# Few-row products become transfers, transposes or zero-padded products; meta keys turned four heads at a time

## The chip, the cores and the metric

The kernel runs on one core of a Trainium2 chip. The metric is device microseconds of one execution. A core has TensorE (PE in the profile; its weight loads are PEld), VectorE (DVE), ScalarE (ACT), GpSimd (POOL) and SyncE (SP); transfers are issued from the queues of SP, POOL and ScalarE.

## What is computed

The reference is a small model on one sequence: 256 tokens behind 16 meta tokens, width 1024, all in float32. Four blocks follow one another, each with a residual: (1) an attention with 16 heads of 64 over a window of 128 keys plus the 16 meta keys and a sink; (2) a gated delta rule with 8 key heads and 16 value heads of 128, run in chunks, so that the 16 meta tokens give a first state for the 256 others; (3) a mixer of a differential attention (4 heads) and a windowed attention (8 query heads on two heads of keys and values, seeing the meta keys too); (4) a SwiGLU feed-forward. In short:

```python
h = concat(meta_tokens, x)
h = h + attention_mixer(h, ...)          # block 1
h = h + deltanet_mixer(h, ...)           # block 2
h = concat(meta_tokens_2, h[16:])
h = h + mixer_block(rms_norm(h), ...)    # block 3
h = h + swiglu(rms_norm(h), ...)         # block 4
return rms_norm(h)[16:]
```

## The kernel before

Activations lie transposed, with 128 features on the partitions and the 272 tokens along the free dimension. Weights come from HBM in pieces (`raw`), and each piece is split into a high part (`hi`, written by ScalarE) and a low part (`lo`, written by VectorE); a projection is three fast products per piece (`mm3`), into the PSUM banks `mm`. These products are most of TensorE's work (the names `mm<-U,hi` and `mm<-U,lo` in the profile). All other products are plain float32, through `Plan.mm` into the PSUM banks `aux`, where one product is two TensorE instructions; a transposition (`Plan.tr`) is one.

Every operation is recorded by a helper (`Plan._rec`, hence one line number, L223, for all), with an estimated duration. `Plan.schedule` then places all operations of the kernel in one order by priority, with an estimate of each engine's time, of buffers and of transfers; `Plan.emit` writes them out in that order, each engine in order. Buffers are rings by tag (`SLOTS`): a tile must be the next of its tag, or at most a few ahead (`AHEAD`), to be placed.

The places that the change touches, in the order of time:

- In `attention`, `V[:, 2, :]` holds the values of the 16 meta tokens (16 rows), and `VM` is to hold them once for each of two query blocks and two heads, shifted to rows 32b + 16e, so that one product with 128 rows serves a pair of heads (`pair`). Before, eight instructions with 16-row operands shift them, with a selection matrix `sel`, through PSUM.
- In `meta`, the attention of the 16 meta queries: the scores are products over 64 rows (one half of the partitions for each of two key heads), and the output is a product over 16 rows.
- In `gates`, `rstd` (the same in every row) is brought into token order by 1-row products with `self.unity`, and the cumulative sums of the gates of the meta tokens are products over 16 rows (`gt0`). The sums go to HBM (`mem<-row`) and come back to all partitions (`U<-mem`, `gb`), for `decays`.
- In `key_norms`, the scaled betas of the meta tokens (`br0`, 16x16) are transposed into `brow`.
- In `tokens(j)`, the keys of head j are transposed; the meta keys too, and then copied to two places of `kt0` with a scale for each head (16 copies of 16x128 in all). `first_states` multiplies `kt0` by `U0`, the inverses for the meta tokens, into `W0`, which each head's first product reads. In the order, `tokens` lie between 190 and 287 us, `first_states` beside the merges of the block inverses (`merge`) near 290 us.
- In `second_mixer`, `VM` is built as in the first attention, with two pairs of 16-row instructions.

Of the kernel before, what the change touches and what calls it, by code (L numbers as in the profile page):

```python
# [10 lines left out]
F32 = mybir.dt.float32  # L11
# [7 lines left out]
NM = 16  # L19
# [112 lines left out]
class Plan:  # L132
# [337 lines left out]
class Net:  # L470
# [10 lines left out]
    def constants(self):  # L481
# [17 lines left out]
        self.unity = self.eps[0:1, 2:3]  # L499
# [169 lines left out]
    def attention(self, h):  # L669
# [20 lines left out]
        V = p.tile([128, 3, 128], F32, "x1")  # L690
        vps = p.bank("aux")
# [6 lines left out]
        sel = p.tile([16, 4, 64], F32, "c")  # L698
        p.memset(sel, 0.0)
        VM = p.tile([128, 2, 128], F32, "vm")  # L700
        p.memset(VM, 0.0)
        for b in range(2):
            mps = p.bank("aux")
            for e in range(2):
                q = 2 * b + e
                p.copy(sel[:, q, 32 * b + 16 * e:32 * b + 16 * e + 16], self.ident[0:16, 0:16])
                p.mm(mps[0:64, 64 * e:64 * e + 64], sel[:, q, :], V[0:NM, 2, 64 * e:64 * e + 64])
            p.act(VM[0:64, b, :], mps[0:64, 0:128], AF.Copy)
# [38 lines left out]
        def meta():  # L747
            biasm = p.tile([128, 2, NM], F32, "c")
            p.dma(biasm, a["bias_m"], 16384, "gpsimd", after=(keys,))
            qm = p.tile([128, 8, NM], F32, "c")  # L750
            p.copy(qm, qT[:, :, 0:NM])
            t = p.tile([128, 2, NM], F32, "c")
            for e in range(2):
                es = slice(64 * e, 64 * e + 64)
                sps = p.bank("aux")[:, 0:NM]
                p.mm(sps, qm[es].rearrange("p j t -> p (j t)"), kT[es, 0:NM])
                p.tt(t[:, e, :], sps, biasm[:, e, :], ALU.add)
# [18 lines left out]
            pm = p.tile([NM, 256], F32, "x1")  # L776
            p.act(pm, pps[0:NM, 0:256], AF.Copy)
            ops = p.bank("aux")
            for e in range(2):
                ec = slice(64 * e, 64 * e + 64)  # L780
                p.mm(ops[ec, 0:128], V[0:NM, 2, ec], pm[:, 128 * e:128 * e + 128])
# [76 lines left out]
    def deltanet(self, h):  # L858
# [73 lines left out]
        id16 = self.ident[0:16, 0:16]  # L932
        beta, g = [p.tile([128, 3, 16], F32, "t3") for _ in range(2)]
        bt, bt0, gt, gt0 = beta[:, 0:2, :], beta[0:NM, 2, :], g[:, 0:2, :], g[0:NM, 2, :]
# [25 lines left out]
        for t in (U0, kt0):  # L960
            p.memset(t, 0.0)
# [6 lines left out]
        def gates():  # L968
# [18 lines left out]
            for t, (t0, w) in enumerate(KEY_TILES):  # L987
                p.mm(ps[0:w, 32 * t:32 * t + 32], rows[:, t0:t0 + w], fold)
                if t < 2:
                    p.mm(ps[:, 96 + t:97 + t], rstd[0:1, t0:t0 + w], self.unity)  # L990
# [3 lines left out]
            p.act(rt, ps[:, 96:98], AF.Copy)  # L994
# [23 lines left out]
            p.mm(ps[0:16, 32:48], triu[0:16, 0:16], gt0)  # L1018
# [5 lines left out]
            p.mm(ps[0:16, 0:NM], gt0, triu[0:16, 0:16])  # L1024
# [50 lines left out]
        def key_norms():  # L1075
# [4 lines left out]
            br, br0 = tok(), tok0()  # L1080
# [715 lines left out]
```

## Time and profile before

| | |
|---|---|
| median of 3 runs | 812.78 us (812.3 to 814.78) |
| the profiled execution | 811.36 us, with a span of 809.2 us |
| TensorE busy | 778.0 us, 96% of the span |
| VectorE, ScalarE, POOL busy | 610.0 (75%), 539.7 (67%), 38.0 us (5%) |
| granted TensorE clock, mean | 0.994 of full speed |

The span goes from the first to the last instruction. A busy TensorE is not TensorE at its peak, since products overlap: one of 272 columns is shown with 0.29 us, and the next one starts 0.12 us after it. A row of the profile names what is written, an arrow, and what is read, with buffer numbers left out; `16*64 16x64` are the shapes of weights and of the moving operand. The chain of waits is followed back from the last instruction, at each step to what released it or to the instruction before it on its engine.

### The profile page before, as it was taken

The page shows a single profiled execution, that of the slowest core. Times are in us where ns is not written, and L with a number is a line of the kernel's source. Part 1 is how long each engine was busy: PE and PEld are TensorE (multiplying, and loading weights), DVE is VectorE, ACT ScalarE, POOL GpSimd, SP SyncE. Part 2 cuts the span into 40 slices and gives each one's busy share as a digit, 9 for nine tenths or more (in the row PEclk, how much of TensorE's full clock was granted, in tenths as well). Part 3 has the DMA queues.
Part 4 walks back from the last instruction along what each step waited for, and adds up shares of the span by engine and source line. Part 5 has one row for each costly group of instructions (what it writes and reads, how often), then busy time and mean ns, then how long its engine had stood idle before and what let it go on. Part 6 is the DMA issues. An engine that isn't in the chain of part 4 may idle for free.

```text
span 809.2 us, 16346 instructions
## 1 busy us (share of the span) xinstructions
PE 778.0 (96%) x5994; PEld 718.9 (89%) x5994; DVE 610.0 (75%) x1522; ACT 539.7 (67%) x1239; POOL 38.0 (5%) x106
## 2 busy tenths in 40 slices
PE   7999989979999999999999899999999999999996
PEld 6999978867889998988999898899999899999995
DVE  6699975899999956887668589877958666656554
ACT  7689876988865646997557478886548645344333
POOL 3100011001000010000012000000000000000000
PEclk9999999989999999999999999999999999999999
DMA  7736445544765643222656955446665775655611
GB/s 225 220 87 205 149 144 187 170 150 111 232 184 165 183 118 119 55 80 66 178 179 185 218 160 168 167 134 205 183 183 182 214 231 184 202 185 176 204 64 52
DMA packets 52847, 131.55 MB, mean 163 GB/s; under 512 B 17232, under 2 KB 21040, under 8 KB 52512
## 3 DMA queue, kind: packets, MB, share of 16 engines
q1 hardware_dynamic: 48752, 122.42, 49.1%
q0 software_dynamic: 3584, 7.55, 3.5%
q8 instruction: 47, 0.77, 0.4%
q10 hardware_dynamic: 432, 0.54, 0.2%
q14 instruction: 32, 0.26, 0.1%
HBM read 123.98 MB, written 4.85 MB: 159 GB/s over the span
## 4 chain that ended last, share of the span: by engine, by line
PE 78%; ACT 8%; DVE 6%; DMA 5%; issue 2%; SPq 0%; ACTq 0%; DVEq 0%
PE mm L223 49%; PE aux L223 29%; DVE U L223 2%; ACT L223 2%; ACT hi L223 2%; DMA raw<-w_c_dram 1%; ACT U L223 1%; DMA raw<-w_u_dram 1%; DVE lo L223 1%; DMA U<-mem 1%; DVE sys L223 1%; ACT sys L223 1%; ACT o L223 1%; DMA U<-x_dram 1%; DMA raw<-w_b_dram 0%
## 5 line engine op out<-in xcount | busy, mean ns | idle before, releaser
L223 PE MATMUL mm<-U,hi 128*128 128x272 f32 (+2 forms) x1728 | 332.9, 293 | 7.5 <-ACT hi L223 6.1
L223 PEld LDWEIGHTS mm<-U,hi 128*128 128x128 f32 x1728 | 266.5, 190 | 16.3 <-ACT hi L223 9.5
L223 ACT ACTIVATE hi<-raw 128x512 fp32r<-128x512 f32 x280 | 171.7, 626 | 99.1 <-PE mm L223 78.7
L223 DVE TENSOR_TENSOR lo<-raw,hi 128x512 fp32r<-128x512 f32 x280 | 191.1, 692 | 54.8 <-ACT hi L223 51.0
L223 PE MATMUL mm<-U,lo 128*128 128x272 f32 (+2 forms) x864 | 227.4, 293 | 0.7 <-DVE lo L223 0.7
L223 PE MATMUL aux<-U 128*128 128x256 f32 (+6 forms) x1392 | 193.7, 272 | 0.8 <-ACT kt L223 0.5
L223 PEld LDWEIGHTS aux<-U 128*128 128x128 f32 (+4 forms) x1392 | 172.5, 180 | 8.0 <-issue 2.0
L223 PEld LDWEIGHTS mm<-U,lo 128*128 128x128 f32 x864 | 155.1, 189 | 3.4 <-DVE lo L223 1.9
L223 ACT ACTIVATE U<-raw 128x1024 fp32r<-128x1024 f32 x66 | 69.5, 1055 | 55.9 <-PE aux L223 37.9
L223 DVE TENSOR_TENSOR U<-raw,U 128x1024 fp32r<-128x1024 f32 x66 | 80.5, 1221 | 19.4 <-ACT U L223 18.5
L223 PE MATMUL mm<-U,oh 128*128 128x512 f32 x176 | 64.0, 395 | 0.4 <-ACT sys L223 0.4
L223 DVE TENSOR_TENSOR c<-aux,rstd 128x256 f32<-128x256 f32 x44 | 18.6, 422 | 40.2 <-PE aux L223 40.0
L223 DVE SCALAR_TENSOR_TENSOR c<-c,vec 128x272 f32<-128x272 f32 (+1 forms) x97 | 46.9, 494 | 1.7 <-ACT c L223 0.9
L223 PE MATMUL mm<-oh,hi 128*128 128x256 f32 x256 | 46.5, 286 | 0.0
L223 ACT ACT_TABLE_LOAD x30 | 38.5, 1283 | 3.7 <-DMA U<-x_dram 3.2
L223 PE MATMUL mm<-hi,U 128*128 128x512 f32 x128 | 40.1, 405 | 0.0
L223 PEld LDWEIGHTS mm<-oh,hi 128*128 128x128 f32 x256 | 38.1, 188 | 0.1
L223 PEld LDWEIGHTS mm<-U,oh 128*128 128x128 f32 x176 | 32.0, 188 | 5.5 <-ACT sys L223 0.9
L223 ACT ACTIVATE sys<-sys,sm 128x272 f32<-128x272 f32 x64 | 30.9, 486 | 3.3 <-DVE sm L223 3.3
L223 PE MATMUL mm<-oh,lo 128*128 128x256 f32 x128 | 31.7, 280 | 0.0
L223 ACT ACTIVATE oh<-c 128x256 fp32r<-128x256 f32 x22 | 9.1, 415 | 29.8 <-DVE c L223 29.7
L223 PEld LDWEIGHTS mm<-hi,U 128*128 128x128 f32 x128 | 23.2, 188 | 4.4 <-issue 0.4
(257 smaller groups left out, 1069.7 us busy)
## 6 DMA issues: line engine op xcount, KB each, us to landing
raw<-w_c_dram SPq DMA_DIRECT2D x34, 512.0 KB, 3.7
raw<-w_b_dram SPq DMA_DIRECT2D x32, 512.0 KB, 3.7
raw<-w_g_dram SPq DMA_DIRECT2D x22, 512.0 KB, 4.6
raw<-w_u_dram SPq DMA_DIRECT2D x22, 512.0 KB, 4.5
raw<-w_d_dram SPq DMA_DIRECT2D x22, 512.0 KB, 3.7
raw<-w_a_dram SPq DMA_DIRECT2D x17, 512.0 KB, 3.9
raw<-w_bz_dram SPq DMA_DIRECT2D x16, 512.0 KB, 4.3
raw<-w_bo_dram SPq DMA_DIRECT2D x16, 512.0 KB, 3.6
```

What stands on the lines that cost most here:

```text
L223: return getattr(getattr(self.nc, attr), fn)(*[real(v) for v in args], **{n: real(v) for n, v in kw.items()})
```

## The change

`VM` is filled by transfers inside SBUF on POOL's queue (four in the attention, two in the second mixer) instead of through products with `sel`. The meta queries are put into two zeroed tiles, one for each key head, and the products use all 128 rows; so does the output product, with zeroed rows in `V` and `pm`. In the gates, `rstd` is transposed whole (128x128) and one column of it read; the cumulative sums of the meta gates use 128 rows, those beyond 16 meeting zeros of `triu`. `br0` gets 128 rows, zeroed beyond 16. The meta keys are turned in `first_states` instead of `tokens`: `kx` (zeroed, from the ring `M`) takes the keys of four heads at a time, one transposition gives 128 rows with head q at rows 32q, and one copy with a scale by row (`elgq`) writes them to `kt0`.

```diff
@@ -448,7 +448,7 @@
 SLOTS = {
     "mm": 4, "aux": 4,
     "U": 11, "M": 3, "sys": 2, "raw": 3, "hi": 5, "lo": 5, "c": 8, "sq": 4, "rstd": 1, "sm": 8, "x1": 2,
-    "mask": 2, "tok": 26, "o1": 2, "row": 2, "t3": 6, "ba": 1, "m0": 3, "bsys": 1, "fold": 1,  "u0": 1, "tmp": 2, "bv": 2, "bv0": 2, "kt0": 1, "vm": 1, "sums": 1, "w0": 1, "ktok": 1, 
+    "mask": 2, "tok": 26, "o1": 2, "row": 2, "t3": 6, "ba": 1, "m0": 3, "bsys": 1, "fold": 1,  "u0": 1, "tmp": 2, "bv": 2, "bv0": 2, "kt0": 1, "vm": 1, "sums": 1, "w0": 1, "elgq": 1, "ktok": 1, 
     "S": 2, "vn": 2, "vs": 2, "r": 2, "oh": 4, "V0": 1, "lam": 4,
 }
 
@@ -496,7 +496,6 @@
         p.memset(self.eps[:, 1:2], 64 * EPS)
         p.memset(self.eps[:, 2:3], 1.0)
         p.memset(self.eps[:, 3:4], -0.5)
-        self.unity = self.eps[0:1, 2:3]
 
         self.pick = self.const("pick", [128, 64])
         p.memset(self.pick, 0.0)
@@ -688,6 +687,7 @@
         vT = p.tile([128, T], F32, "c")
         p.tt(vT, self.project(a["w_a"][:, 1], x), rstd, ALU.mult)
         V = p.tile([128, 3, 128], F32, "x1")
+        p.memset(V[:, 2, :], 0.0)
         vps = p.bank("aux")
         for i, (t0, n) in enumerate(KEY_TILES):
             p.tr(vps[0:n, i * 128:(i + 1) * 128], vT[:, t0:t0 + n], self.ident)
@@ -695,17 +695,12 @@
         p.act(V[0:NM, 2, :], vps[0:NM, 256:384], AF.Copy)
 
 
-        sel = p.tile([16, 4, 64], F32, "c")
-        p.memset(sel, 0.0)
         VM = p.tile([128, 2, 128], F32, "vm")
         p.memset(VM, 0.0)
         for b in range(2):
-            mps = p.bank("aux")
             for e in range(2):
-                q = 2 * b + e
-                p.copy(sel[:, q, 32 * b + 16 * e:32 * b + 16 * e + 16], self.ident[0:16, 0:16])
-                p.mm(mps[0:64, 64 * e:64 * e + 64], sel[:, q, :], V[0:NM, 2, 64 * e:64 * e + 64])
-            p.act(VM[0:64, b, :], mps[0:64, 0:128], AF.Copy)
+                q, ec = 32 * b + 16 * e, slice(64 * e, 64 * e + 64)
+                p.dma(VM[q:q + NM, b, ec], V[0:NM, 2, ec], 4096, "gpsimd")
 
         qT = p.tile([128, 8, T], F32, "U")
         qss = p.tile([128, 8, T], F32, "U")
@@ -747,13 +742,14 @@
         def meta():
             biasm = p.tile([128, 2, NM], F32, "c")
             p.dma(biasm, a["bias_m"], 16384, "gpsimd", after=(keys,))
-            qm = p.tile([128, 8, NM], F32, "c")
-            p.copy(qm, qT[:, :, 0:NM])
             t = p.tile([128, 2, NM], F32, "c")
             for e in range(2):
                 es = slice(64 * e, 64 * e + 64)
+                qm = p.tile([128, 8, NM], F32, "c")
+                p.memset(qm, 0.0)
+                p.copy(qm[es], qT[es, :, 0:NM])
                 sps = p.bank("aux")[:, 0:NM]
-                p.mm(sps, qm[es].rearrange("p j t -> p (j t)"), kT[es, 0:NM])
+                p.mm(sps, qm.rearrange("p j t -> p (j t)"), kT[:, 0:NM])
                 p.tt(t[:, e, :], sps, biasm[:, e, :], ALU.add)
             m = p.tile([128, 4], F32, "sm")[:, 0:2]
             e0 = p.tile([128, 4], F32, "sm")[:, 0:2]
@@ -773,12 +769,13 @@
             pps = p.bank("aux")
             for e in range(2):
                 p.tr(pps[0:NM, 128 * e:128 * e + 128], t[:, e, :], self.ident)
-            pm = p.tile([NM, 256], F32, "x1")
-            p.act(pm, pps[0:NM, 0:256], AF.Copy)
+            pm = p.tile([128, 256], F32, "x1")
+            p.memset(pm, 0.0)
+            p.act(pm[0:NM], pps[0:NM, 0:256], AF.Copy)
             ops = p.bank("aux")
             for e in range(2):
                 ec = slice(64 * e, 64 * e + 64)
-                p.mm(ops[ec, 0:128], V[0:NM, 2, ec], pm[:, 128 * e:128 * e + 128])
+                p.mm(ops[ec, 0:128], V[:, 2, ec], pm[:, 128 * e:128 * e + 128])
             p.act(om, ops[:, 0:128], AF.Copy)
 
         def pair(j):
@@ -929,9 +926,8 @@
             return v.rearrange("p (j e) -> p j e", e=2)
 
         row = lambda: p.tile([16, T], F32, "row")
-        id16 = self.ident[0:16, 0:16]
         beta, g = [p.tile([128, 3, 16], F32, "t3") for _ in range(2)]
-        bt, bt0, gt, gt0 = beta[:, 0:2, :], beta[0:NM, 2, :], g[:, 0:2, :], g[0:NM, 2, :]
+        bt, bt0, gt = beta[:, 0:2, :], beta[0:NM, 2, :], g[:, 0:2, :]
         gc, gc0, gr, brow = tok(), tok0(), row(), row()
         eg, elg, elg0 = tok(), p.tile([128, 16], F32, "tok"), tok0()
         egl = p.tile([128, 16], F32, "tok")
@@ -957,8 +953,7 @@
         ktok = p.tile([128, 8, 128], F32, "ktok")
         kt0 = p.tile([128, 4, 128], F32, "kt0")
         W0 = p.tile([128, 4, 128], F32, "w0")
-        for t in (U0, kt0):
-            p.memset(t, 0.0)
+        p.memset(U0, 0.0)
         xh, xl = x
         done = {}
 
@@ -987,11 +982,11 @@
             for t, (t0, w) in enumerate(KEY_TILES):
                 p.mm(ps[0:w, 32 * t:32 * t + 32], rows[:, t0:t0 + w], fold)
                 if t < 2:
-                    p.mm(ps[:, 96 + t:97 + t], rstd[0:1, t0:t0 + w], self.unity)
+                    p.tr(ps[:, 128 + 128 * t:256 + 128 * t], rstd[:, t0:t0 + w], self.ident)
             t3 = lambda: p.tile([128, 3, 16], F32, "t3")
             ba = p.tile([128, 3, 32], F32, "ba")
             p.memset(ba, 0.0)
-            p.act(rt, ps[:, 96:98], AF.Copy)
+            p.act(rt.unsqueeze(2), ps[:, 128:384].rearrange("p (t c) -> p t c", t=2)[:, :, 0:1], AF.Copy, n=2)
             p.act(ba[:, 0:2, :].rearrange("p n h -> p (n h)"), ps[:, 0:64], AF.Copy, n=64)
             p.act(ba[0:NM, 2, :], ps[0:NM, 64:96], AF.Copy)
             p.act(beta, ba[:, :, 0:16], AF.Sigmoid, n=48)
@@ -1015,13 +1010,13 @@
             ps = p.bank("aux")
             for n in range(2):
                 p.mm(ps[:, 16 * n:16 * n + 16], triu, gt[:, n, :])
-            p.mm(ps[0:16, 32:48], triu[0:16, 0:16], gt0)
+            p.mm(ps[0:16, 32:48], triu[:, 0:16], g[:, 2, :])
             p.act(gc.rearrange("p n h -> p (n h)"), ps[:, 0:32], AF.Copy, n=32)
             p.act(gc0, ps[0:16, 32:48], AF.Copy)
             ps = p.bank("aux")
             for n in range(2):
                 p.mm(ps[0:16, NM + 128 * n:NM + 128 * n + 128], gt[:, n, :], triu)
-            p.mm(ps[0:16, 0:NM], gt0, triu[0:16, 0:16])
+            p.mm(ps[0:16, 0:NM], g[:, 2, :], triu[:, 0:16])
             p.act(gr, ps[0:16, 0:T], AF.Copy)
 
             scr_g = p.tile([16, T], F32, None, "dram")
@@ -1077,15 +1072,17 @@
             done["rk0"] = rk0 = rsqrt_small(ssk0, self.eps[0:NM, 0:1], [16, 8], -0.5 * EPS)
 
 
-            br, br0 = tok(), tok0()
+            br, br0 = tok(), p.tile([128, 16], F32, "tok")
+            p.memset(br0, 0.0)
             for n in range(2):
                 p.tt(heads2(br, n), heads2(bt, n), by_head(rk, n), ALU.mult, n=16)
-            p.tt(heads2(br0), heads2(bt0), by_head(rk0), ALU.mult, n=16)
+            p.tt(heads2(br0[0:NM]), heads2(bt0), by_head(rk0), ALU.mult, n=16)
             ps = p.bank("aux")
             for n in range(2):
                 p.tr(ps[0:16, NM + 128 * n:NM + 128 * n + 128], br[:, n, :], self.ident)
-            p.tr(ps[0:16, 0:NM], br0, id16)
-            p.act(brow, ps[0:16, 0:T], AF.Copy)
+            p.tr(ps[0:16, T:T + 128], br0, self.ident)
+            p.act(brow[:, NM:T], ps[0:16, NM:T], AF.Copy)
+            p.act(brow[:, 0:NM], ps[0:16, T:T + NM], AF.Copy)
             scr_b = p.tile([2, 16, 128], F32, None, "dram")
             for n in range(2):
                 p.dma(scr_b[n], brow[:, NM + 128 * n:NM + 128 * n + 128], 8192, "sync")
@@ -1182,16 +1179,23 @@
         def tokens(j):
             ps = p.bank("aux")
             p.tr(ps[:, 0:128], kT[:, j, NM:NM + 128], self.ident)
-            p.tr(ps[0:NM, 128:256], kT[:, j, 0:NM], self.ident)
             p.act(ktok[:, j, :], ps[:, 0:128], AF.Copy)
+
+        def first_states():
+
+            kx = p.tile([128, 4, 4, 32], F32, "M")
+            p.memset(kx, 0.0)
             for e in range(2):
-                h_ = 2 * j + e
-                q = 32 * (h_ % 4)
-                p.act(kt0[q:q + NM, j // 2, :], ps[0:NM, 128:256], AF.Copy, scale=elg0[:, h_:h_ + 1])
-
-        def first_states():
-
+                p.copy(kx.rearrange("p g (i e) c -> p g i e c", e=2)[:, :, :, e, 0:NM],
+                       kT[:, :, 0:NM].rearrange("p (g i) c -> p g i c", i=2), n=128)
+            elgq = p.tile([128, 4], F32, "elgq")
+            p.memset(elgq, 0.0)
+            for q in range(4):
+                p.copy(elgq[32 * q:32 * q + NM], elg0.rearrange("p (g q) -> p q g", q=4)[:, q, :], n=4)
             for g_ in range(4):
+                ps = p.bank("aux")[:, 0:128]
+                p.tr(ps, kx[:, g_].rearrange("p q c -> p (q c)"), self.ident)
+                p.act(kt0[:, g_, :], ps, AF.Copy, scale=elgq[:, g_:g_ + 1])
                 ps = p.bank("aux")[:, 0:128]
                 p.mm(ps, U0[:, g_, :], kt0[:, g_, :])
                 p.act(W0[:, g_, :], ps, AF.Copy)
@@ -1412,15 +1416,11 @@
             p.act(V[:, :, i, :], ps[:, 0:256].rearrange("p (n d) -> p n d", n=2), AF.Copy)
             p.act(V0[0:NM, i, :], ps[0:NM, 256:384], AF.Copy)
 
-        sel = p.tile([16, 2, 32], F32, "c")
-        p.memset(sel, 0.0)
         VM = p.tile([128, 2, 128], F32, "vm")[:, 0]
         p.memset(VM, 0.0)
-        mps = p.bank("aux")
         for e in range(2):
-            p.copy(sel[:, e, 16 * e:16 * e + 16], self.ident[0:16, 0:16])
-            p.mm(mps[0:32, 64 * e:64 * e + 64], sel[:, e, :], V0[0:NM, 4, 64 * e:64 * e + 64])
-        p.act(VM[0:32], mps[0:32, 0:128], AF.Copy)
+            ec = slice(64 * e, 64 * e + 64)
+            p.dma(VM[16 * e:16 * e + NM, ec], V0[0:NM, 4, ec], 4096, "gpsimd")
         for i in range(8):
             q = p.tile([128, T], F32, "c")[:, 0:S]
             p.stt(q, self.project(a["w_c"][:, 10 + i], x, NM), 0.125, rq, ALU.mult, ALU.mult)
```

## Rows read from the trace of the kernel before

**Rows 1.** Busy time in three stretches: us of each engine (instructions), TensorE clock, DMA share, GB/s.

```profile
40.00:60.00 20.00, 19.54 (x149) 18.66 (x148) 19.39 (x59) 17.73 (x44) 0.00 (x0) 1.00 0.31 86
...
188.00:198.00 10.00, 9.30 (x64) 7.10 (x63) 9.79 (x30) 8.53 (x18) 3.23 (x6) 1.00 0.37 99
282.00:306.00 24.00, 23.80 (x451) 21.71 (x450) 14.16 (x27) 11.84 (x26) 2.74 (x7) 1.00 0.42 117
```

**Rows 2.** Timeline of TensorE near 38 us: start, us, what, merged count, idle before.

```profile
37.52 0.29 PE L223 MATMUL mm<-U,lo 128*128 128x272 f32 x1
37.64 0.41 PE L223 MATMUL mm<-U,hi 128*128 128x272 f32 x2
37.98 0.32 PE L223 MATMUL aux<-x,c 16*64 16x64 f32 x2
38.24 0.52 PE L223 MATMUL mm<-U,hi 128*128 128x272 f32 x2
```

**Rows 3.** The chain that ended last, 36 to 66 us: start, us, what.

```profile
38.05 0.25 PE aux L223 x2
...
38.88 0.25 PE aux L223 x2
...
40.09 0.37 PE aux L223 x4
...
57.93 0.23 DVE c L223
...
61.46 0.33 PE aux L223 x3
```

**Rows 4.** DMA issues by tile and queue: count, KB each, median us to landing.

```profile
bv<-bv POOLq DMA_DIRECT2D x4, 68.0 KB, 6.4
```

**Rows 5.** Readers of tile `vm`: whole span, then 440 to 540 us (ns min/median/max, starts).

```profile
L223 PE MATMUL aux<-pad,vm x40: 272/275/483, 60.1 to 538.2; 128*128 128x128 f32 x32, 128*128 128x256 f32 x8
...
L223 PE MATMUL aux<-pad,vm x8: 377/379/483, 514.7 to 538.2; 128*128 128x256 f32 x8
```

**Rows 6.** Timeline of TensorE in the gates.

```profile
135.38 0.29 PE L223 MATMUL mm<-U,hi 128*128 128x272 f32 x1
135.60 0.60 PE L223 MATMUL aux<-eps,rstd 1*128 1x1 f32 x4
136.13 0.39 PE L223 MATMUL mm<-U,hi 128*128 128x272 f32 x1
```

**Rows 7.** Writers of tile `kt0` (shown as `kt`) on ScalarE.

```profile
L223 ACT ACTIVATE kt<-aux,tok x16: 342/358/359, 193.9 to 286.5; 16x128 f32<-16x128 f32 x16
```

**Rows 8.** Timelines of ScalarE, TensorE and POOL, 190 to 197 us.

```profile
193.94 0.73 ACT L223 ACTIVATE kt<-aux,tok 16x128 f32<-16x128 f32 x2 [1.05 <-DVE tok L223]
...
194.72 0.49 PE L223 MATMUL aux<-U 128*128 128x128 f32 x2 [0.46 <-ACT kt L223]
...
191.11 1.80 POOL L223 MEMSET U<- 128x2048 f32 x1
192.86 0.95 POOL L223 MEMSET sys<- 128x1024 f32 x1
```

**Rows 9.** VectorE's instructions on `tok` tiles, 185 to 200 us (ns min/median/max).

```profile
L223 DVE TENSOR_TENSOR tok<-tok x5: 149/175/1243, 187.6 to 196.3; 128x16 f32<-128x16 f32 x2, 16x8 f32<-16x8 f32 x1, 16x16 f32<-16x16 f32 x1, 128x32 f32<-128x32 f32 x1
```

**Rows 10.** Timeline of TensorE in the second mixer.

```profile
474.15 0.29 PE L223 MATMUL aux<-ktok,c 16*32 16x64 f32 x2
474.38 0.39 PE L223 MATMUL aux<-U 128*128 128x272 f32 x1
474.70 0.29 PE L223 MATMUL aux<-ktok,c 16*32 16x64 f32 x2
474.93 0.39 PE L223 MATMUL aux<-U 128*128 128x272 f32 x1
```

**Rows 11.** Timeline of TensorE: the wait that ends at 164.87 us.

```profile
164.87 1.34 PE L223 MATMUL mm<-U,hi 128*128 128x260 f32 x4 [3.95 <-ACT hi L223]
```

**Rows 12.** Busy time by stretch, the two us after that wait (columns as in rows 1).

```profile
165.00:167.00 2.00, 1.78 (x6) 1.28 (x6) 2.00 (x10) 2.00 (x5) 0.00 (x0) 0.51 0.00 0
```

## The prediction

> **What bounds the kernel now.** I first read the busy time by stretch. TensorE runs through most of the span, and three stretches show how the parts this change touches differ [rows 1]. From 40 to 60 us VectorE is busy 19.39 of 20 us and ScalarE 17.73: there TensorE's work comes as fast as they let it. From 188 to 198 us VectorE is again the fullest (9.79 of 10). From 282 to 306 us TensorE is busy 23.80 of 24 and VectorE only 14.16. So a microsecond off TensorE is worth most in the third kind of place, and a microsecond off ScalarE or VectorE in the others.
>
> Then I read the timeline of TensorE around the few-row products. In the stream of projections a product starts every 0.12 to 0.13 us (37.52, then 37.64) [rows 2]. Two such are merged in the row at 37.64, so the next would start at 37.89. Instead come two 16-row products at 37.98, and the stream goes on at 38.24: the pair cost 0.35 us, where two more products of the stream would have cost 0.25. The chain of waits has the same pair on it with 0.25 us, and two more groups like it with 0.25 and 0.37 [rows 3]. So these products are small but sit on the path, and each group costs about 0.1 us more than its own piece of the chain.
>
> **The change part by part.** The sum is made against the profiled execution's own 811.36 us (a span of 809.2 and 2.16 around it). The median of the runs is 812.78, 1.42 higher, so I add 1.42 at the end.
>
> (a) Meta values of the first attention. Eight TensorE instructions, two PSUM copies on ScalarE and four VectorE copies become four 4 KB transfers on POOL's queue. On the chain the eight take 0.25 + 0.25 + 0.37 = 0.87 us [rows 3]; by the gaps in the stream 0.1 us more for each of three groups, 1.17 us. Behind them the stage is VectorE's (19.39 of 20) [rows 1], so part of this is given back as waiting: bounds 0 and -1.17, and I take -0.7, nearer to the chain's own figure. The transfers cost nothing while they land in time. POOL's nearest transfers inside SBUF, 68 KB each, took a median of 6.4 us [rows 4]. The values exist by 37.98 us, where the first few-row product reads them [rows 2], and the first product that reads the transferred ones starts at 60.1 us [rows 5], so there are 22 us of cover. Were it gone, pair 0's output product would wait and the softmax stage behind it with it, for as long as the transfer is late.
>
> (b) The attention of the meta queries. The products with 64 and 16 rows keep their number and their columns, so I let their TensorE time stand. The masked queries now need a copy for each half instead of one; the present one takes 0.23 us and is on the chain [rows 3]. Added +0.2 (bounds 0 and +0.45, if both copies and their zeroing came late).
>
> (c) Column sums to token order in the gates. Four 1-row instructions start at 135.60; the product before them starts at 135.38 and could be followed at 135.50; the stream goes on at 136.13 [rows 6]. That is 0.63 us. Two transposes take their place; three transposes took 0.33 us on the chain, 0.11 each [rows 3], so 0.22. Gain 0.4 (bound 0, if ScalarE's chain of the gates hides it).
>
> (d) The cumulative gates of the meta tokens use 128 rows instead of 16, with the same number of instructions and columns: nothing. (e) The zero-padded transposition of the scaled betas saves a switch and adds one short ScalarE copy and one POOL memset: 0, with +0.3 as the bound.
>
> (f) Meta keys. Eight small transposes become four, 4 x 0.11 = 0.44 us of TensorE. Sixteen ScalarE copies of 0.358 us [rows 7] become four of the same width: 12 x 0.358 = 4.3 us of ScalarE. Most of it lies in stretches where ScalarE is not the last to come. At 193.94 it does lie on the path: two of these copies hold ScalarE for 0.73 us after an idle 1.05, and TensorE idles 0.46 for them [rows 8]. I take the 0.73, so -0.4 - 0.7 = -1.1 (bounds -0.44 and -2.2 with the whole 1.05).
>
> (g) What comes in its place stands ahead of the first states: a zeroing of 128x512, two VectorE copies, four very small ones, four transposes and four ScalarE copies. VectorE's part is about 2 x 0.23 [rows 3] and 4 x 0.175 [rows 9], 1.2 us; ScalarE's is in (f). It is covered by the merges, where VectorE has 9.8 us free of 24 [rows 1]. Cost 0; without that cover 1.2, and 0.5 more if the zeroing holds the copies up: +1.7. The zeroed tile takes a third of the ring that the merges use too, so a late release would show as a wait of a merge.
>
> (h) Meta values of the second mixer. Two pairs of 16-row instructions at 474.15 and 474.70; the stream goes on at 474.38 and 474.93 [rows 10]. The second pair takes from 474.50 (one step after 474.38) to 474.93, 0.43 us; the first 0.23 and the gap ahead of it, about 0.3. TensorE carries the chain there, so -0.7 (bound 0). The transfers have until 514.7 us [rows 5].
>
> Sum: -0.7 + 0.2 - 0.4 - 1.1 - 0.7 = -2.7. 811.36 - 2.7 + 1.42 = **810.1 us**. With every gain at its small end and every cost at its large one (+2.45, less the 0.44 of the transposes) it is 814.8, with all gains at the large end (-1.17 - 0.4 - 2.2 - 0.74 = -4.5) 808.3.
>
> A rule speaks against this reading. The Trainium skill (TensorE: Matmul & The Clock Gate, "Why this matters for your kernels") says that a single product of 32 rows takes the same time as one of 128, so that rows are only worth something when several run at once. By it the groups would cost 0.25 us for a pair rather than 0.35 to 0.43, and the gain of (a) and (h) would be about 0.5 us smaller, 810.6 in all; the rows at 37.98 and 474.70 do not follow it.
>
> **Rivals.**
> *The work was off the path (no change).* If VectorE and ScalarE set the first attention and the stretch at 190 us, (a) and (f) give nothing beyond 0.44, and 812.78 + 0.2 - 0.4 - 0.44 - 0.7 = 811.4 remains, within 0.3%. For it: 19.39 of 20 and 9.79 of 10 [rows 1]; against it: the groups stand on the chain [rows 3].
>
> *VectorE stands behind POOL (slower).* The padded betas need zeroed rows, and the zeroing can be placed only when its buffer comes round, at about 191 us. There POOL has a memset of 1.80 us from 191.11 and one of 0.95 from 192.86 [rows 8]. If the zeroing is queued behind them, VectorE's instruction on those rows, one of the operations of [rows 9], waits for at most 2.7 us; I price it at 2.3, for an instruction due soon after the first of them starts. VectorE stands still for it, and with it the splits of weights queued on VectorE, and TensorE runs dry. That POOL's memsets can hold VectorE there is seen already: one operation of 0.175 us median took 1.243 while they ran [rows 9]. The Trainium skill (SBUF — State Buffer, "Who interferes with whom") puts such a thing down to a port pair that the two engines lock in turn; the row agrees with it. If TensorE then idles as long as at 160.9 to 164.9 (3.95 us), its clock falls too: after that wait the granted clock is 0.51 of full speed, the 1.2 GHz level [rows 11, 12], for three rows of 2 us and part of a fourth, which loses up to 3.2 us. Price 2.3 + 3.2 = 5.5, so 810.1 + 5.5 = 815.6. It decides from 5.1 us on (2.7 to eat up the gain, 2.4 to be seen). The same price holds if the order, which is worked out anew for all instructions, opens such a hole elsewhere. Against it: TensorE idled only 0.46 us when VectorE was held for 1.2.
>
> *The wait at 161 us closes (faster still).* The broadcast rows of the gates end it. If (c) brings them earlier and the clock stays up, up to 3.2 us come back: 806.9.
>
> *The change does nothing there.* The products are gone by construction, so only the price of each can be wrong; this is in the first rival.
>
> **How the numbers follow.** Likeliest, the sum: 0.50, with a range of its own of 808.3 to 811.6. Off the path 0.18, VectorE behind POOL or another hole 0.20, the wait at 161 closing 0.12. A measurement tells 0.3% (2.4 us), so faster means below 810.3 and slower above 815.2. Of the sum's 0.50 I put 0.33 below 810.3; with the 0.12 faster is 0.45. The slower rival gives 0.16 above 815.2, the rest of it stays within. Same: 0.17 + 0.18 + 0.04 = 0.39. The range runs from 806.5 (the closed wait) to 815.0 (just short of the hole); some 0.06 lie below, 0.14 above.
>
> **What would show it.** After the change: in the stream near 38 to 40 us no gap of 0.35; no 16-row copies of `kt` on ScalarE and 4 of 128 rows near 285 us, with no wait of TensorE for them; the second mixer's stream without gaps near 473 us; POOL with six more transfers. Wrong would be: a wait of a product on a transfer into `vm`; VectorE idle for POOL near 191 us; a new TensorE hole of over 2 us; a merge or a head waiting on the first states.

## The result, and the profile after

The changed kernel takes 806.96 us (median; 806.55 to 807.9), the kernel before 812.7 us beside it: ratio 0.9925, 95% interval [0.9905, 0.9944]. A second measurement with more executions gave 0.9933 [0.9917, 0.9948], 5.4 us. The prediction's 810.1 us had the direction, and its range (806.5 to 815.0 us) held the time by half a microsecond, but the gain is twice its 2.7 us.

First TensorE where few-row work stood, by timelines of the kernel after (start, us, what, count): the projections near 38 us, the gates, and the hole that is left in the second mixer.

```profile
37.46 0.55 PE L223 MATMUL mm<-U,hi 128*128 128x272 f32 x3
37.85 0.29 PE L223 MATMUL mm<-U,lo 128*128 128x272 f32 x1
37.97 0.29 PE L223 MATMUL mm<-U,hi 128*128 128x272 f32 x1
...
134.47 0.29 PE L223 MATMUL mm<-U,hi 128*128 128x272 f32 x1
134.60 0.38 PE L223 MATMUL aux<-ident,rstd 128*128 128x128 f32 x2
134.74 0.37 PE L223 MATMUL mm<-U,hi 128*128 128x272 f32 x1
...
452.34 0.51 PE L223 MATMUL mm<-U,hi 128*128 128x256 f32 x2 [0.63 <-ACT hi L223]
```

The stream near 38 us runs on at 0.12 to 0.13 us a product where [rows 2] had a gap. The two transposes in the gates take 0.14 us of the stream (134.60 to 134.74) where [rows 6] had 0.63. What replaced the products in the meta values, by the DMA issues (KB each, median us to landing), and then by tile the readers of those and the copies of the meta keys (ns min/median/max, first and last start):

```profile
vm<-x POOLq DMA_DIRECT2D x4, 4.0 KB, 4.3
vm<-ktok POOLq DMA_DIRECT2D x2, 4.0 KB, 2.2
```

```profile
L223 PE MATMUL aux<-pad,vm x40: 270/275/483, 58.7 to 534.0; 128*128 128x128 f32 x32, 128*128 128x256 f32 x8
...
L223 ACT ACTIVATE kt<-aux,elgq x4: 360/368/368, 285.7 to 291.0; 128x128 f32<-128x128 f32 x4
```

The transfers land in 4.3 and 2.2 us, and the first reader starts at 58.7 us with no wait for them, as [rows 5] allowed. The sixteen copies of [rows 7] are four of the same width, now in the middle of the merges. The same three stretches as [rows 1]:

```profile
40.00:60.00 20.00, 17.98 (x120) 16.98 (x119) 19.48 (x66) 16.18 (x41) 0.00 (x0) 0.88 0.25 78
188.00:198.00 10.00, 10.00 (x63) 8.67 (x61) 9.62 (x25) 4.66 (x10) 3.23 (x6) 1.00 0.36 76
282.00:306.00 24.00, 22.67 (x362) 20.74 (x359) 10.76 (x21) 12.28 (x28) 2.75 (x7) 1.00 0.33 109
```

Three things stand in them that the removed instructions alone do not give: from 40 to 60 us TensorE is busy 1.6 us less and its mean granted clock is down to 0.88; around 190 us ScalarE fell from 8.53 to 4.66 us, of which the removed copies are 1.5, and TensorE no longer waits at all; and in the merges TensorE lost 1.1 us. The first and the last are holes of TensorE. Timelines of ScalarE at the first, and of TensorE at both:

```profile
50.83 1.28 ACT L223 ACT_TABLE_LOAD   x1
...
54.32 1.65 ACT L223 ACTIVATE hi<-raw 128x512 fp32r<-128x512 f32 x3
...
54.99 0.52 PE L223 MATMUL mm<-U,hi 128*128 128x272 f32 x2 [2.02 <-ACT hi L223]
...
285.76 1.12 PE L223 MATMUL aux<-U 128*64 128x64 f32 x16 [1.33 <-issue]
```

A table load and the exponentials of the first pair now stand ahead of a split of weights, and TensorE idles 2.02 us for that split; the hole is 2.01 or 2.02 us long in all six profiles that have it. The hole near 285 us is of another kind: in a second execution of the same kernel it is 0.38 us (experiment 3). So the whole change is new instructions and a new order, and the experiments take the two apart.

The table gives the length of each stage in one profiled execution per kernel, from the starts of the same instructions in the timelines: ScalarE's four writes of `rstd` (they divide start, attention, deltanet, mixer and the last part), its first copy into `row` (the end of the gates) and VectorE's last operation of the big solve. The kernels of the second and third row issue the sequence of the kernel before up to the second mixer, so down to there the first three rows show how far one order scatters. The two stages around the end of the solve are best read together: 277.81 and 277.46 us in the changed kernel, 278.74, 277.44 and 277.34 in the first three rows.

| kernel | start | attention | to `row` | to end of solve | to end of deltanet | mixer | last part |
|---|---|---|---|---|---|---|---|
| before | 12.72 | 120.17 | 17.89 | 117.38 | 161.36 | 186.40 | 193.28 |
| same order (mixer: transfers) | 13.12 | 119.76 | 17.88 | 116.01 | 161.43 | 184.99 | 193.01 |
| same order (mixer: reordered) | 12.83 | 119.77 | 17.87 | 115.92 | 161.42 | 188.18 | 193.21 |
| new work, old order | 13.73 | 119.22 | 17.34 | 118.13 | 163.35 | 185.39 | 193.24 |
| old work, new order | 12.25 | 119.70 | 17.87 | 118.38 | 162.33 | 187.45 | 193.42 |
| after | 12.18 | 120.11 | 17.04 | 113.98 | 163.83 | 184.53 | 193.13 |
| after, second execution | 11.96 | 119.29 | 17.25 | 114.60 | 162.86 | 186.70 | 192.84 |

### The profile page after: what moved, and what is told of

Its sections match the earlier page's. It is cut to its first block, busy times and chain, and to the rows that moved or that the text cites. A ratio compares the mean times of both kernels' runs of the same rounds, so it can differ in the third digit from the quotient of the medians.

```text
span 804.8 us, 16307 instructions
## 1 busy us (share of the span) xinstructions
PE 775.7 (96%) x5976; PEld 719.1 (89%) x5976; DVE 608.3 (76%) x1523; ACT 531.2 (66%) x1223; POOL 41.4 (5%) x116
## 4 chain that ended last, share of the span: by engine, by line
PE 84%; ACT 6%; DMA 4%; DVE 4%; issue 2%; SPq 0%; ACTq 0%; DVEq 0%
PE mm L223 53%; PE aux L223 31%; ACT L223 1%; DVE U L223 1%; DMA U<-mem 1%; DMA raw<-w_c_dram 1%; ACT hi L223 1%; ACT U L223 1%; DVE lo L223 1%; DMA raw<-w_u_dram 1%; DVE sys L223 1%; ACT bv L223 1%; ACT sys L223 1%; DMA U<-x_dram 1%; ACT o L223 0%
## 5 line engine op out<-in xcount | busy, mean ns | idle before, releaser
L223 DVE TENSOR_TENSOR lo<-raw,hi 128x512 fp32r<-128x512 f32 x280 | 189.3, 685 | 58.7 <-ACT hi L223 54.0
L223 PE MATMUL aux<-U 128*128 128x256 f32 (+5 forms) x1392 | 193.7, 272 | 2.2 <-issue 1.3
L223 PEld LDWEIGHTS aux<-U 128*128 128x128 f32 (+3 forms) x1392 | 172.6, 180 | 9.4 <-issue 3.0
L223 ACT ACTIVATE U<-c 128x272 f32<-128x272 f32 (+4 forms) x58 | 24.2, 420 | 8.4 <-DVE c L223 7.9
```

The source lines that it names most:

```text
L223: return getattr(getattr(self.nc, attr), fn)(*[real(v) for v in args], **{n: real(v) for n, v in kw.items()})
```

## The experiments

All are ratios to the kernel before on the same chip; microseconds are the ratio times its median there (811.9 to 812.6).

**1. Each part alone.** The three parts of the diff, each put into the kernel before (one pair of lines of each is shown, the rest of the code is left out).

```diff
 # keys: tokens() and first_states(), as in the diff of the change
-            p.tr(ps[0:NM, 128:256], kT[:, j, 0:NM], self.ident)
+                p.tr(ps, kx[:, g_].rearrange("p q c -> p (q c)"), self.ident)
 ...
 # transfers: both builds of VM
-                p.mm(mps[0:64, 64 * e:64 * e + 64], sel[:, q, :], V[0:NM, 2, 64 * e:64 * e + 64])
+                p.dma(VM[q:q + NM, b, ec], V[0:NM, 2, ec], 4096, "gpsimd")
 ...
 # padding: everything else
-                    p.mm(ps[:, 96 + t:97 + t], rstd[0:1, t0:t0 + w], self.unity)
+                    p.tr(ps[:, 128 + 128 * t:256 + 128 * t], rstd[:, t0:t0 + w], self.ident)
```

Keys alone: 

> Only the meta keys are turned four heads at a time (in the step of the first states); everything else as before. If the price of the work decides, as the prediction has it, this part is worth 1.1 us: ratio to before 0.9986, ScalarE without the sixteen 16-row copies near 190 us, and the stage of the merges unchanged. If the order that the scheduler rebuilds around it decides, the ratio is anywhere between 0.995 and 1.005 and the span's gain or loss stands at places that hold none of the edited instructions.

Transfers alone: 

> Only the two builds of the meta values' matrix become transfers (attention and second mixer). Price of the work: 0.7 + 0.7 us, ratio 0.9983, with the holes near 38 to 40 us and near 474 us gone and nothing else moved. Rebuilt order: the product streams differ after 40 us too, and the ratio is off that by more than 1 us either way; the wait for DMA or VectorE near 456 us would change without being touched.

Padding alone: 

> Only the padded operands and the transposes for the rstd column: meta queries, meta products, triu gates, the row of beta. Price of the work: +0.2 - 0.4, ratio 0.9998, the same as before. Rebuilt order: more than 1 us either way. If the three parts alone add up to the whole change's 5.7 us within 1 us, the parts are independent and the work is the likelier cause; if their sum is off by more than 2 us, the order is.

Measured: keys 1.0035 [1.0017, 1.0053], 2.8 us *slower*; transfers 0.9951 [0.9934, 0.9968], 4.0 us faster; padding 0.9991 [0.9978, 1.0004], 0.7 us. The sum is -1.9 where the whole gives -5.4. (The expectations of later runs quote the three as differences of medians: +3.5, -3.4 and -0.9 us.) The keys, which the prediction had as the largest gain, cost; the transfers gave almost three times their price.

One place where the keys alone lose, by the timelines of TensorE, ScalarE and SP in that kernel:

```profile
287.58 0.33 PE L223 MATMUL aux<-ident,M 128*128 128x128 f32 x1 [1.88 <-ACT U L223]
...
285.76 1.15 ACT L223 ACTIVATE hi<-raw 128x512 fp32r<-128x512 f32 x2 [4.03 <-PE aux L223]
286.94 1.81 ACT L223 ACTIVATE U<-aux 32x512 f32<-32x512 f32 x3
288.78 0.63 ACT L223 ACTIVATE kt<-aux,elgq 128x128 f32<-128x128 f32 x2
...
281.81 6.66 SPq L223 DMA_DIRECT2D raw<-w_b_dram  x4
```

Just ahead of the new transposes ScalarE stands 4.03 us at a split of weights; three copies of the merges are queued behind it, and TensorE idles 1.88 us for the first. The row names TensorE as what ended ScalarE's wait, but SP had issued these weights only 3.95 us before, about what such a transfer takes to land (a median of 4.0 us in the changed kernel), so a late transfer is the likelier cause. From `row` to the end of the deltanet this kernel takes 281.04 us against 277.34 to 278.74 in the first three rows of the table. The hole is a part of this; where the rest goes is not shown.

**2. Work and order crossed.** The program's order is a list that the planner makes anew for every edit. Here the list of one kernel is imposed on the operations of the other.

```diff
         self.order = order
+        keys = ...   # positions taken from the other kernel, left out here
+        self.order = [(float(i), self.ops[k]) for i, k in enumerate(keys)]
```

New work in the old order: 

> The changed kernel's instructions, issued in the order of the kernel before: each engine takes the instructions that both kernels share in exactly the old sequence (two neighbours on TensorE and one on VectorE swapped), the new ones stand where the replaced ones stood or where their operands are ready, and the buffer kx has memory of its own so that the old order stays possible. If the price of the work decides: most of the 5.7 us, ratio 0.9930 to 0.9967 (2.7 to 5.7 us). If the rebuilt order decides: a ratio of 0.998 to 1.001.

Old work in the new order: 

> The other half: the instructions of the kernel before, issued in the order of the changed kernel (one swap on each engine); the few-row ones stand where their replacements stand or where their operands are ready. If the price of the work decides: nothing, ratio 0.998 to 1.002. If the rebuilt order decides: 0.993 to 0.997 (2.7 to 5.7 us faster without a single instruction changed).

Measured: 0.9987 [0.9973, 1.0001], 1.1 us faster, and 1.002 [1.0008, 1.0033], 1.6 us slower. Both theories fall: neither half holds the gain. The table shows why the new work gets so little in the old order. The attention (119.22 against 119.76 to 120.17), the gates (17.34 against 17.88) and the mixer (185.39 against 186.40) are shorter by 0.7, 0.5 and 1.0 us; but up to the end of the solve 1.7 us are lost against the mean of the first three rows, and behind it 1.95. The first loss, by TensorE, VectorE and POOL there:

```profile
194.81 0.79 PE L228 MATMUL aux<-U 128*128 128x128 f32 x2 [1.93 <-DVE U L228]
...
191.42 1.43 DVE L228 TENSOR_SCALAR tok<-tok 128x32 f32<-128x32 f32 x1
191.51 1.34 DVE L228 TENSOR_TENSOR tok<-tok 16x16 f32<-16x16 f32 x1
192.96 0.68 DVE L228 COPY elgq<-tok 16x4 f32<-16x4 f32 x4
193.67 0.69 DVE L228 TENSOR_TENSOR lo<-raw,hi 128x512 fp32r<-128x512 f32 x1
...
190.08 1.80 POOL L228 MEMSET U<- 128x2048 f32 x1
191.83 0.95 POOL L228 MEMSET sys<- 128x1024 f32 x1
```

VectorE is held for 1.4 us while POOL writes, the four new `elgq` copies add 0.68, and a split of weights follows; TensorE's wait there grew from 0.46 [rows 8] to 1.93 us, and the mean granted clock from 185 to 205 us is 0.91. In the changed kernel's own order the `TENSOR_SCALAR` comes before POOL's memsets (at 187.24 us, 0.16 us long), the `elgq` copies at 197.6 us, and TensorE waits for nothing there. Where the new instructions stand in the old order was chosen for this kernel, so this loss belongs to that choice as much as to the old order.

**3. The ring of buffers.**

```diff
-            kx = p.tile([128, 4, 4, 32], F32, "M")
+            kx = p.tile([128, 4, 4, 32], F32, "kx")
```

> The changed kernel with the padded meta keys (kx) in memory of their own instead of in one of the three buffers of the ring that the merges use; the scheduler gives the same order. In the changed kernel two of the merges' memsets on GpSimd now run at 289 and 291 us, in the middle of the merges, and about 4 us of the lead are given back there. If the ring is what gives them back, this kernel is 1.5 to 4 us faster than the changed one (803 to 805.5 us, ratio 0.988 to 0.991) and the hole of 1.33 us on TensorE near 284.4 us is gone. If the transposes and copies of the first states themselves do it, it stays at 806 to 807.5 us (0.992 to 0.994).

Measured: 0.9945 [0.9928, 0.9962], no faster than the changed kernel. The hole of 1.33 us is gone and the stretch behind the solve takes 162.50 us (163.83 and 162.86 in the changed kernel). But this is not shown to be the ring's doing, since the hole shrinks without any edit. SP, ScalarE and TensorE in the changed kernel's first execution, then in its second:

```profile
280.53 8.16 SPq L223 DMA_DIRECT2D raw<-w_b_dram  x4
...
284.42 0.63 ACT L223 ACTIVATE hi<-raw 128x512 fp32r<-128x512 f32 x1 [1.40 <-DMA raw<-w_b_dram]
285.07 0.59 ACT L223 ACTIVATE U<-aux 32x512 f32<-32x512 f32 x1
```

```profile
279.62 7.92 SPq L223 DMA_DIRECT2D raw<-w_b_dram  x4
...
283.27 0.63 ACT L223 ACTIVATE hi<-raw 128x512 fp32r<-128x512 f32 x1 [0.44 <-DMA raw<-w_b_dram]
...
284.61 1.12 PE L223 MATMUL aux<-U 128*64 128x64 f32 x16 [0.38 <-issue]
```

The product that TensorE waits with starts 0.1 us after a copy of the merges, and that copy stands on ScalarE behind a split of weights that land late. The weights were issued 0.52 us ahead of ScalarE's first copy of the merges in the first execution, 1.23 in the second and 1.50 in the kernel with `kx` by itself, whose TensorE, ScalarE and VectorE have the same sequence; the holes are 1.33, 0.38 and none. So the ring is not where the lead goes, and this hole is a wait for a transfer that differs from execution to execution.

**4. Two parts at a time, and the hole at 53 us.** The changed kernel again, without its keys, without its transfers, and with its attention alone in the old order.

> The changed kernel once more, as the yardstick for the three others on the same chip. Ratio to before 0.9905 to 0.9944 as measured first.

Without the keys: 

> The change without its third part: transfers for the meta values and padded or turned operands, but the meta keys turned head by head as before. The three parts alone gave +3.5 (keys), -3.4 (transfers) and -0.9 us (padding), together -0.8 where the whole gave -5.7. If the keys cost about 3 us in any company, this kernel is 0.9888 to 0.990 (803 to 805 us) and faster than the changed one. If the parts act on one another through the order that is rebuilt, the keys' cost is not there in this company and it stands at 0.9935 to 0.997 (807.5 to 810 us), slower than the changed one.

Without the transfers: 

> The change without the transfers: the meta values keep their selecting products. If the parts add up, 1.0026 (keys +0.35%, padding -0.09%). If they act on one another, it lies below that by more than 2 us: 0.996 to 0.9995.

Old order in the attention: 

> The changed kernel's instructions in the changed kernel's order, except that in the attention (up to some 130 us) the shared instructions stand in the order of the kernel before. The changed order puts a table load and the four exponentials of the first pair ahead of a split of weights on ScalarE, TensorE idles 2.02 us at 53 us and its granted clock falls to 0.88 and 0.94 in the next 40 us; the old order has neither. If that hole and the slow clock behind it cost what they show, this kernel is 2.0 + 3.5 us faster than the changed one: 801 to 804 us, ratio 0.987 to 0.989. If VectorE bounds these pairs (busy 19.5, 19.7 and 19.0 of 20 us in the three slices from 40 us in the kernel before), the attention takes as long either way and the time stays at 806 to 808.5 us (0.992 to 0.995).

Measured: again 0.9933 [0.9917, 0.9948]; without the keys 0.9938 [0.9922, 0.9955]; without the transfers 1.0001 [0.9989, 1.0013]; old order in the attention 0.9948 [0.9928, 0.9968]. So transfers and padding alone have the whole gain: the keys add 0.4 us to it, good to 1.8 and so nothing that can be told, though alone they cost 2.8 us. Without the transfers nothing is left. The hole at 53 us and the slow clock behind it cost nothing that can be told: with both gone the time is not lower, where 5.5 us were on offer. The reading of the stretches in that kernel, to be held against the first of those shown above:

```profile
40.00:60.00 20.00, 18.87 (x143) 18.11 (x142) 19.55 (x63) 17.33 (x42) 1.21 (x5) 1.00 0.34 97
60.00:80.00 20.00, 20.00 (x165) 18.18 (x164) 19.72 (x77) 18.18 (x61) 1.72 (x4) 1.00 0.60 207
```

VectorE is busy 19.55 and 19.72 of 20 us with TensorE at full clock; in the changed kernel TensorE waits and runs slow, and the attention takes 120.11 and 119.29 us against 119.04 here. That fits VectorE as the bound of these pairs, as [rows 1] had it.

**5. The second mixer by itself.** Everything before 429 us is issued as in the kernel before.

```diff
 # transfers: only the second mixer's VM, as in the diff of the change
 ...
 # reordered: the same work, only
-        sel = p.tile([16, 4, 64], F32, "c")
+        sel = p.tile([16, 4, 64], F32, "sel")
-        sel = p.tile([16, 2, 32], F32, "c")
+        sel = p.tile([16, 2, 32], F32, "sel2")
```

> Only the second mixer's matrix of meta values is built by transfers; the order of every instruction up to the second mixer is that of the kernel before, and the mixer's own order is that of the changed kernel. The two transfers together (attention and second mixer) gave 3.4 us where the prediction had 1.4. If each is worth its removed instructions, this one gives 0.7 us (ratio 0.9991) and the hole of 2.64 us near 457 us stays. If the mixer's rebuilt order is where the rest comes from, the hole falls to 0.6 to 1.3 us and the ratio is 0.997 to 0.998 (1.6 to 2.4 us); the attention's transfers are then left with 1 to 2 us.

> No instruction of the kernel before is removed or replaced: only the two selecting matrices get memory of their own instead of one of the eight shared buffers, which lets the scheduler rebuild the second mixer's order (74 neighbours change places on TensorE) and leaves all before it as it was. If a rebuilt order alone is worth what the transfers gave in the mixer, because the shared buffer comes free, the ratio is 0.997 to 0.998 and the hole near 457 us is shorter. If the removal itself is needed, 0.999 to 1.001; a loss (above 1.001) would say that an order rebuilt at random is as likely to lose.

Measured: transfers 0.9971 [0.9955, 0.9987], 2.4 us; reordered without any removal 0.9989 [0.9973, 1.0006], not told from nothing. ScalarE, VectorE and TensorE in the kernel before, then ScalarE and TensorE with the mixer's transfers:

```profile
454.96 1.15 ACT L223 ACTIVATE hi<-raw 128x512 fp32r<-128x512 f32 x2 [2.82 <-DMA raw<-w_c_dram]
...
455.62 0.69 DVE L223 TENSOR_TENSOR lo<-raw,hi 128x512 fp32r<-128x512 f32 x1 [3.02 <-ACT hi L223]
456.23 0.43 DVE L223 TENSOR_TENSOR c<-mm,rstd 128x272 f32<-128x272 f32 x1
...
456.72 0.55 PE L223 MATMUL aux<-ident,c 128*128 128x128 f32 x3 [2.64 <-DVE c L223]
```

```profile
453.18 1.15 ACT L223 ACTIVATE hi<-raw 128x512 fp32r<-128x512 f32 x2 [2.96 <-DMA raw<-w_c_dram]
...
453.86 0.50 PE L223 MATMUL mm<-U,hi 128*128 128x256 f32 x2 [1.11 <-ACT hi L223]
```

ScalarE waits for a weight transfer in both. Before, TensorE's next instruction in line was a transpose of values. It needs nothing of the late weight: the products behind its values were issued before the wait, the last at 453.80 us. But VectorE writes those values (456.23) only behind the low half of that weight (455.62) in its own queue, and so the transpose waits for the split, the low half and the operation behind it: 2.64 us. In the new order the next projection stands there and needs only the high half, out 0.68 us after the weights land: 1.11, and 0.22 for the low half. That is 1.3 us. The reordered kernel kept the transpose there and a wait of 2.27 us.

The other profiles side with this. The six kernels with the transpose in that place (before, reordered, keys alone, padding alone, keys and padding, new work in the old order) wait 2.03 to 3.27 us, 2.6 on average. The eight executions with the projection there (the changed kernel twice, transfers alone, the mixer's transfers, `kx` by itself, without the keys, old order in the attention, old work in the new order) wait 0.85 to 1.89 us, 1.4 on average. The difference is some 1.2 us. Old work in the new order has the shorter wait too, 1.89 us, but pays for it 20 us on, where its few-row products now stand ahead of data that are not ready:

```profile
476.16 0.41 PE L228 MATMUL aux<-ktok,c 16*32 16x64 f32 x4 [1.00 <-ACT ktok L228]
```

So in the mixer the new order pays only where the few-row products are gone.

## Why the prediction was right or wrong

**That the range held the time was luck.** The sum's own range ended at 808.3 us, above the measured 806.96. What reached down to 806.5 was the rival in which the wait at 161 us closes (806.9), and that wait did not close. The time got there by other ways: the mixer's wait, and a part that is not located.

**The prices of the few-row instructions held.** With the order held, (c) gave 0.5 us in the gates (the working had 0.4), and (a) and (b) together 0.7 in the attention (0.5): 119.22 and 119.04 us in two profiles against 119.76 to 120.17. For (h) the stage as a whole is no measure, so I take the stretch from the transpose behind the wait near 457 us to the one that ends the wait near 491: 33.97 us in the kernel before, 33.92 in the padding kernel, which leaves the mixer as it was, and 33.12 with the new work in the old order. That is 0.8 us (0.7). So [rows 3, 6, 10] were read rightly. Whole stages scatter more, between executions of equal order: the mixer by 2.2 us (184.53 and 186.70 in the changed kernel), the stage up to the end of the solve by 1.4, the attention by 0.4 in the old order and by 5 in the new one (119.29 to 124.56, the last in the kernel of experiment 3, where VectorE waited 3.21 us for a transfer of biases).

**The term of (h) was mis-sized.** The mixer's transfers are worth 2.4 us [1.1, 3.7] and not 0.7. The rest fits the wait near 457 us, which the working did not look at and which the new order shortens by some 1.2 us. It could have been seen as a wait for a transfer, with an instruction in line behind it whose values were held up in another engine's queue, while its neighbour could go on.

**What (a) is worth can't be told.** Both transfers together gave 4.0 us, so about 1.6 is left for the attention's, against 0.7; it is a difference of two ratios, good to some 2 us. Where it would come back is not settled: with the old order in the attention the changed kernel was 0.9948 against 0.9933, within the measurement, and old work in the new order gained nothing there.

**(f) and (g) failed where they stand alone.** The step was "Cost 0" for the additions under cover of the merges, with a gain of 1.1 for the copies. Alone the keys cost 2.8 us, past the 1.3 that the bounds allow (-0.44 and +1.7). In the changed kernel they are worth 0.4 us, good to 1.8, which decides neither for the 1.1 nor for nothing. The cover was read from busy time, 9.8 us free on VectorE [rows 1]; but the additions did not lack busy time. In the old order the `elgq` copies stood ahead of the multiplies of the systems. In the kernel with the keys alone, the rebuilt order put splits of late weights ahead of the copies of the merges, 1.88 us of its loss; the rest of that loss is open.

**(d), (e) and the copies of (b)** can't be told apart; the padding altogether gives 0.7 us [-0.3, 1.8]. It does bring the `row` copy 0.5 us nearer with the order held, and 0.6 to 0.8 in the changed kernel.

**What the sum left out** is that every instruction is placed anew. 2.4 us for the mixer's transfers, 1.6 for the attention's, 0.7 for the padding and, beside these, 0.4 for the keys make 5.1 of 5.4 us; with terms good to 1 to 2 us each, this says only that they are compatible. Some 2 us are the price of the instructions (0.7, 0.5 and 0.8). Of the rest only the mixer's wait, 1.2 us, is shown at its place. New work in the old order gives 1.1 us and old work in the new order loses 1.6, so neither carries the gain by itself; that the remainder needs both is argued from this and shown in the mixer alone.

**What was to show it.** The gap near 38 us, the 16-row copies and the gaps in the mixer are gone, and no product waits for a transfer into `vm`. One of the signs against it did come: a new hole of over 2 us, which cost nothing that can be told; that VectorE sets the pace there fits. The hole of 1.33 us beside the first states looked like another, but it is a wait for weights and was 0.38 us in the next execution.

**The rivals.** "Off the path" is not decided for the keys at 194 us, whose hole of 0.46 us is gone while their worth can't be told, and was wrong for the mixer. "VectorE behind POOL" did not come about. The zeroing was not held until 191 us, as the rival had it, but done at 154.10, and VectorE's operations were placed ahead of POOL's memsets (the operations of [rows 9] by tile, ns min/median/max, and the timelines of POOL and VectorE):

```profile
L223 DVE TENSOR_TENSOR tok<-tok x5: 149/156/174, 184.7 to 188.4; 128x16 f32<-128x16 f32 x2, 16x8 f32<-16x8 f32 x1, 16x16 f32<-16x16 f32 x1, 128x32 f32<-128x32 f32 x1
```

```profile
154.10 0.11 POOL L223 MEMSET tok<- 128x16 f32 x1
...
189.03 1.80 POOL L223 MEMSET U<- 128x2048 f32 x1
...
189.48 2.81 DVE L223 SCALAR_TENSOR_TENSOR U<-aux,tok,U 128x256 f32<-128x256 f32 x7
```

The slowest of them is 174 ns instead of 1243. New work in the old order did have a hole of 1.93 us at the very place, but not by the zeroing (at 155.51 us there): VectorE was held as in the kernel before, 1.43 against 1.32 us, and the `elgq` copies came on top. "The wait at 161 us closes" did not happen: it is 3.40 and 0.53 us, and 3.38 and 0.53 in a kernel whose order there is the old one.

## What to carry to other kernels

Where a planner orders the program, price an edit at the waits near it as well as at its instructions: for each wait on a transfer ask which instruction stands next in line, whether it needs the late data, and whether what it does need stands behind the late data in another engine's queue. Free busy time on an engine is no cover for work that enters its queue; look at what stands behind the added instruction. Before a hole is put down to an edit, look for it in a second execution of the same kernel. And test a part in the company in which it will run, and again with the order held: here a part that cost 2.8 us alone cost nothing that could be told beside the others, and work and order were each worth little without the other.

## What the runs showed of the hardware

The clock after the same wait differed between executions of the same instructions. The first of two stretches is from the kernel before, after TensorE idled 3.95 us [rows 11]; the second is from the kernel with the mixer's transfers, which differs from it only after 429 us, after waits of 3.38 and 0.53 us (columns as in [rows 1]):

```profile
164.00:172.00 8.00, 6.74 (x26) 5.89 (x27) 7.93 (x24) 5.83 (x16) 0.00 (x0) 0.57 0.46 147
```

```profile
164.00:172.00 8.00, 7.17 (x43) 6.75 (x44) 7.93 (x24) 6.72 (x15) 0.00 (x0) 0.79 0.56 192
```

The mean granted clock is 0.57 in the one and 0.79 in the other, means of the 1.2 GHz level (0.5) and the 2.4 GHz level, and the stretch up to the end of the solve takes 117.38 against 116.01 us. So 1.4 us of the lead that the changed kernel's profile shows there (0.79 as well) cannot be put down to the change.

The hold of VectorE by POOL falls, in these rows, on one kind of instruction. With new work in the old order a `TENSOR_SCALAR` of 128x32 took 1.43 us beside POOL's memsets and its successor 1.34; both end 0.07 us after the second memset. In the changed kernel seven operations with one operand in PSUM took 2.81 us together, 0.40 each, beside the memset of 1.80 us, and the same `TENSOR_SCALAR` ahead of it 0.16. The Trainium skill (SBUF — State Buffer, "Who interferes with whom") says that a `tensor_scalar` can enter a mode that takes the port pair which VectorE shares with GpSimd, and that whichever of the two comes second is then blocked for the whole of the other's instruction; an instruction outside such modes with at most one input in SBUF does not contend. The rows agree. In the prediction the delay was read on the successor [rows 9], which only stands behind the blocked one.
